# A hybrid token-mixer block on one core: recurrence products issued by shape and by alternating halves, and the first norm's sums of squares from a token-row copy of the input

## The chip, the cores and the metric

The kernel runs on one NeuronCore of one Trainium2 chip. The metric is device time in microseconds (us), lower is better. Engines are named as the profile names them: PE (TensorE matmul), PEld (its weight loads), DVE (VectorE), ACT (ScalarE), POOL (GpSimd), SP (SyncE, which issues nearly all DMAs).

## What is computed

One layer on x of 256 tokens by 2048 features, all in float32:

```python
h = rms_norm(x, attn_norm)                  # x * rsqrt(mean(x*x)) * g, per token
proj = h @ w_in                             # split into the inputs of four mixers and 4 gates
y_a = gla_mixer(...)                        # chunked gated linear attention
y_b = rglru_mixer(...)                      # conv + gated linear recurrence
y_c = nsa_mixer(...)                        # compressed / selected / window attention
y_d = rwkv7_mixer(...)                      # delta-rule recurrence, 8 heads of 64
merged = sum(sigmoid(gate_n) * (y_n @ w_branch[n]))
x = x + merged @ w_out
x = x + conv_ffn(rms_norm(x, ffn_norm))     # up 2 x 5632, causal conv of 3, silu gate, down
```

The recurrence that the change touches is rwkv7's, which the reference writes token by token and the kernel in four chunks of 64 tokens:

```python
sa = einsum('bhij,bhj->bhi', state, -kk_t)
state = state * w_t + sa[..., None] * (kk_t * a_t) + v_t[..., None] * k_t
y_t = einsum('bhij,bhj->bhi', state, r_t)
```

## The kernel before

Activations lie transposed, features on the 128 partitions and the 256 tokens along the free axis. Weights are streamed once from HBM by SP in pieces `raw` of 128x1024 (512 KB, five buffers). ACT casts each half to a rounded `wh`, DVE forms the rest `wl = raw - wh` (line 328; six buffers each), and `group_A` lets PE multiply both into a PSUM tile `acc`: for each 128-column block one product with 512 moving columns (`acc<-h,wh`) and one with 256 (`acc<-h,wl`). These two are the bulk of the program. The moving side `h` is the input times the norm's gain, split in the same way; the factor 1/rms of each token (`rs`) is multiplied in later, when an accumulator is read out (`scaled`).

The first weight group `r` goes into four PSUM tiles `r` that are read without that factor (`fold`), so `rs` is first needed some products later. `norm_sum` makes it from the pieces `xin` of the transposed input: ACT squares four pieces in place, POOL adds their quarters (lines 423 to 427, `TENSOR_TENSOR` on POOL, recorded under the helper's line 289), and `norm_fin` sums over partitions by a product with ones, takes root and reciprocal, and finally reduces `rs` back to one number per token row (`rstok`).

While the gate and branch products run, the chunks of the recurrence are woven between them. For each chunk `rwkv_pre` makes products `M` (keys against queries, masked into `mt`), and transposes `TK`; `rwkv_chain` makes `G` (from `mt` and `uv`, plus, after the first chunk, from the running state `st`), `U` (the triangular solve `Z` times `G`), `S` (the state update) and `Yo` (the output, again a part from `mt` and a part from `st`). Heads are paired on the partitions: `H` is the two halves 0..63 and 64..127, `j` counts four pairs. The part from `mt` is a product of 128 rows by 64 columns of the array, the part from `st` one of 64 by 64, and `M` one of 64 by 128. GLA has a like product `gy`. The accumulating pair of `G` is written as

```python
for j in range(4):
    for par in range(2):
        self.mm(ps[h, j, :], mt[:, par, j, 0:64], uv[:, j, par, :], start=True, stop=(st is None))
        if st is not None:
            self.mm(ps[h, j, :], ar[h, j, 0, :], st[h, j, :], start=False, stop=True)
```

The order on each engine is set by the framework's scheduler, which simulates a time line from the order of the code and from the bands of `at(...)` ("load" first, then "split", "evac", "mix", "big"). Engines run their queues strictly in that order. In the profile a float32 product of this kind is two matmul records.

Of the kernel before, what the change touches and what calls it, by code (L numbers as in the profile page):

```python
# [11 lines left out]
F32 = mybir.dt.float32  # L12
# [136 lines left out]
def _layout(i):  # L149
    a = {}  # L150
    a["xT"] = np.ascontiguousarray(i["x"][0].T.reshape(16, P, S).transpose(1, 0, 2))
# [74 lines left out]
class Kern:  # L226
# [190 lines left out]
    def norm_sum(self, src, acc=None, sq=None):  # L417

        nc = self.nc
        sq = self.sb("th", [P, 4, 256], F32, "sq") if sq is None else sq  # L420
# [9 lines left out]
    def norm_fin(self, red, tok):  # L430
# [10 lines left out]
        if tok:  # L441
            with self.at("mix"):
                d = self.m1("rsd", 2)
                self.tt(d, rs.rearrange("p (a t) -> p a t", a=2), self.cst("ident").unsqueeze(1).broadcast_to([P, 2, P]), MULT)
                self.rtok = self.sm([P, 2], "rstok")
                nc.vector.tensor_reduce(self.rtok, d, axis=mybir.AxisListType.X, op=ADD)
# [39 lines left out]
    def setup(self):  # L486
# [43 lines left out]
        self.consts = consts  # L530
        return xg
# [242 lines left out]
    def rwkv_pre(self, c, T):  # L774
# [5 lines left out]
        mask = self.cst("mM").unsqueeze(1).broadcast_to([P, 4, 128])  # L780
        for par in range(2):
            h = H[par]
            ps = self.ps("M")
            for j in range(4):
                self.mm(ps[:, j * 128:(j + 1) * 128], bk[h, j, par:par + 2, :].rearrange("p a b -> p (a b)"),
                        ar[h, j, :, :].rearrange("p a b -> p (a b)"))
            self.tt(mt[:, par], ps.rearrange("p (j t) -> p j t", j=4), mask, MULT)
# [14 lines left out]
        if c < 3:  # L802
# [5 lines left out]
            tk = self.sb("m2", [P, 2, 4, 64], F32, "tk")  # L808
            for par in range(2):
                h = H[par]  # L810
                ps = self.ps("TK")[:, 0:256].rearrange("p (j d) -> p j d", j=4)
                for j in range(4):
                    nc.tensor.transpose(ps[:, j, :], ht[h, j, par:par + 2, :].rearrange("p a b -> p (a b)"), idn[h, h])
                nc.scalar.copy(tk[:, par], ps)
# [3 lines left out]
    def rwkv_chain(self, c, T, st):  # L818
# [3 lines left out]
        g4 = lambda n: self.ps(n)[:, 0:256].rearrange("p (j s) -> p j s", j=4)  # L822
        ps = g4("G")
        for j in range(4):
            for par in range(2):
                h = H[par]
                self.mm(ps[h, j, :], mt[:, par, j, 0:64], uv[:, j, par, :], start=True, stop=(st is None))
                if st is not None:
                    self.mm(ps[h, j, :], ar[h, j, 0, :], st[h, j, :], start=False, stop=True)
# [24 lines left out]
        for j in range(4):  # L854
            for par in range(2):
                h = H[par]
                self.mm(ps[h, j, :], uv[:, j, par, :], mt[:, par, j, 64:128], start=True, stop=(st is None))
                if st is not None:
                    self.mm(ps[h, j, :], st[h, j, :], ar[h, j, 1, :], start=False, stop=True)
# [177 lines left out]
    def gla(self):  # L1037
# [28 lines left out]
        for lv in range(8):  # L1066
# [10 lines left out]
            if lv == 6:  # L1077
                for par in range(2):
                    h = H[par]
                    ps = self.ps("gy")[0:64, 0:256].rearrange("p (a t) -> p a t", a=4)  # L1080
                    for j in range(2):
                        for tl in range(2):
                            s0 = tl * 128
                            self.mm(ps[:, 2 * j + tl, :], qe[h, 2 + j, s0:s0 + 64], qe[h, j, s0 + 64:s0 + 128])
                    nc.vector.tensor_copy(st[par][0:64, :, 64:128], ps)
# [289 lines left out]
    def full(self, out):  # L1375
        nc = self.nc
        xg = self.setup()
# [99 lines left out]
        with self.at("evac"):  # L1477
            self.norm_fin(red, False)
# [75 lines left out]
```

## Time and profile before

| | |
|---|---|
| median of 3 runs | 1581.78 us (1580.47 to 1582.03) |
| profiled execution, its own time | 1582.63 us |
| its span on the core | 1580.8 us |
| PE, PEld, DVE, ACT, POOL busy | 99%, 89%, 78%, 61%, 2% of the span |
| TensorE clock granted, mean | 0.991 of full |
| moved by DMA | 305.79 MB, mean 193 GB/s |

The span is what the profiler sees of the core; the execution's own time is 1.83 us longer. Busy shares are means over stages with different limits. A busy PE can be running at half its clock, or be waiting inside itself between products, so its 99% doesn't say that the products take as long as they must.

### The profile page before, as it was taken

The numbers are of one execution on the slowest core, as the hardware profiler recorded it, in microseconds if no ns is written. First come the engines' busy times: TensorE is split into PE (matmuls) and PEld (weight loads), VectorE is DVE, ScalarE is ACT, GpSimd is POOL, SyncE is SP. The second block draws the span as 40 slices with busy tenths as digits, with TensorE's granted clock in tenths as the row PEclk, the third lists the DMA queues.
The fourth block names the chain that finished last, engine by engine and source line by source line (L and its number), as shares of the span: only waits on it lengthen the run. The fifth ranks groups of instructions, "written<-read, shape, count | busy, mean of one in ns | idle before, by whom it ended". The sixth has DMA issues, their size and how long they took to land.

```text
span 1580.8 us, 27481 instructions
## 1 busy us (share of the span) xinstructions
PE 1562.0 (99%) x10062; PEld 1413.0 (89%) x10062; DVE 1238.8 (78%) x2132; ACT 962.7 (61%) x1705; POOL 38.7 (2%) x60
## 2 busy tenths in 40 slices
PE   8999999999899999999999999999999999999998
PEld 7999888888799899899999999999999999999998
DVE  8799986476977677777787888886688886788875
ACT  6787654256665476656665666664466664566653
POOL 3000000000000000000001100000000000000000
PEclk9999999999999999999999999999999999999999
DMA  7756663245456755466676666666666666666664
GB/s 265 242 171 199 203 193 114 75 157 176 154 171 201 275 186 180 148 201 200 201 248 202 204 202 198 208 199 201 200 201 201 201 201 201 202 201 202 200 224 129
DMA packets 95800, 305.79 MB, mean 193 GB/s; under 512 B 20021, under 2 KB 20789, under 8 KB 95664
## 3 DMA queue, kind: packets, MB, share of 16 engines
q1 hardware_dynamic: 94448, 299.60, 59.9%
q0 software_dynamic: 1216, 4.43, 0.8%
q8 instruction: 79, 1.29, 0.3%
q14 instruction: 57, 0.47, 0.1%
HBM read 300.32 MB, written 3.67 MB: 192 GB/s over the span
## 4 chain that ended last, share of the span: by engine, by line
PE 95%; DVE 2%; ACT 1%; issue 1%; DMA 1%; SPq 0%; DVEq 0%; ACTq 0%
PE acc L297 89%; PE G L297 1%; PE Yo L297 1%; DVE wl L328 1%; DVE qe L289 0%; PE M L297 0%; PE no L297 0%; DMA raw<-in_wf_r 0%; PE r L297 0%; PE c L297 0%; ACT wh L327 0%; DVE th L289 0%; PE sc L297 0%; ACT ge L283 0%; PE ptp L1332 0%
## 5 line engine op out<-in xcount | busy, mean ns | idle before, releaser
L297 PE MATMUL acc<-h,wh 128*128 128x512 f32 x3008 | 1001.9, 385 | 3.0 <-DVE th L289 3.0
L327 ACT CAST wh<-raw 128x512 fp32r<-128x512 f32 x1096 | 673.6, 620 | 516.1 <-PE acc L297 490.8
L328 DVE TENSOR_TENSOR wl<-raw,wh 128x512 fp32r<-128x512 f32 x1096 | 757.7, 698 | 278.7 <-ACT wh L327 272.1
L297 PE MATMUL acc<-h,wl 128*128 128x256 f32 x3008 | 826.7, 275 | 0.0
L297 PEld LDWEIGHTS acc<-h,wh 128*128 128x128 f32 x3008 | 571.7, 190 | 85.3 <-DVE th L289 3.5
L297 PEld LDWEIGHTS acc<-h,wl 128*128 128x128 f32 x3008 | 580.5, 193 | 3.8 <-issue 1.6
L297 PE MATMUL acc<-f,wh 128*128 128x512 f32 x704 | 230.7, 382 | 0.0
L297 PE MATMUL acc<-f,wl 128*128 128x256 f32 x704 | 191.9, 273 | 0.0
L297 PEld LDWEIGHTS acc<-f,wh 128*128 128x128 f32 x704 | 133.1, 189 | 18.5
L297 PEld LDWEIGHTS acc<-f,wl 128*128 128x128 f32 x704 | 135.2, 192 | 0.0
L297 PE MATMUL acc<-mg,wh 128*128 128x512 f32 x256 | 83.9, 382 | 0.0
L286 DVE SCALAR_TENSOR_TENSOR u<-u,prm,u 128x254 f32<-128x254 f32 (+1 forms) x176 | 80.8, 480 | 0.5
L297 PE MATMUL acc<-mg,wl 128*128 128x256 f32 x256 | 69.5, 273 | 0.0
L297 PEld LDWEIGHTS acc<-mg,wh 128*128 128x128 f32 x256 | 48.2, 189 | 6.7
L289 DVE TENSOR_TENSOR xres<-xres,acc 128x512 f32<-128x512 f32 (+1 forms) x66 | 44.0, 668 | 10.0 <-PE acc L297 7.9
L283 ACT ACTIVATE u<-u,prm 128x256 f32<-128x256 f32 x88 | 48.1, 594 | 2.7 <-DVE u L289 0.8
L297 PEld LDWEIGHTS acc<-mg,wl 128*128 128x128 f32 x256 | 49.1, 192 | 0.1
L297 PE MATMUL acc<-wh,h 128*128 128x512 f32 (+1 forms) x128 | 32.2, 340 | 0.0
L289 DVE TENSOR_TENSOR u<-u,rs 128x512 f32<-128x512 f32 x44 | 30.1, 684 | 0.0
L289 DVE TENSOR_TENSOR u<-u,acc 128x512 f32<-128x512 f32 x44 | 29.9, 680 | 0.0
L380 ACT COPY u<-acc 128x512 f32<-128x512 f32 x44 | 25.5, 579 | 0.0
L297 PEld LDWEIGHTS acc<-wh,h 128*128 128x128 f32 x128 | 23.2, 202 | 2.1 <-issue 0.4
(399 smaller groups left out, 1240.9 us busy)
## 6 DMA issues: line engine op xcount, KB each, us to landing
raw<-in_w_up SPq DMA_DIRECT2D x176, 512.0 KB, 4.2
raw<-in_w_gate SPq DMA_DIRECT2D x128, 512.0 KB, 4.0
raw<-in_w_down SPq DMA_DIRECT2D x88, 512.0 KB, 4.3
raw<-in_w_branch SPq DMA_DIRECT2D x32, 512.0 KB, 3.8
raw<-in_w_out SPq DMA_DIRECT2D x32, 512.0 KB, 4.4
raw<-in_wf_k SPq DMA_DIRECT2D x8, 512.0 KB, 4.6
raw<-in_wf_misc SPq DMA_DIRECT2D x8, 512.0 KB, 4.0
raw<-in_wf_lx SPq DMA_DIRECT2D x8, 512.0 KB, 4.2
```

What stands on the lines that cost most here:

```text
L283: return self.nc.scalar.activation(out, in_, func, bias=bias, scale=scale, **kw)
L286: return self.nc.vector.scalar_tensor_tensor(out, in0, scalar, in1, op0=op0, op1=op1)
L289: return (eng or self.nc.vector).tensor_tensor(out, a, b, op=op)
L297: return self.nc.tensor.matmul(out, lhsT, rhs, start=start, stop=stop, **kw)
L327: nc.scalar.copy(wh, rb)
L328: nc.vector.tensor_tensor(wl, rb, wh.bitcast(F32), op=SUB)
L380: self.nc.scalar.copy(dst, ps[0:rows, :, 0])
```

## The change

It has two parts, delivered together.

**Order of products.** In `G` and `Yo` all products from `mt` are issued first and all products from `st` after them, instead of in pairs; in `M`, `TK` and `gy` the two halves of the partitions alternate, instead of one half's four products before the other's, so both PSUM tiles of the pair are open at once. The products are the same.

**First norm.** Instead of squaring the transposed pieces on ACT and adding them on POOL, four pieces `xtok` of the input with tokens on the partitions (128x1024 each, 2 MB more from HBM) are loaded, and ACT squares them with a running sum along the row. The root and reciprocal are taken on two numbers per partition; a diagonal matrix of them times ones spreads them to `rs`. The eleven POOL additions of this norm are gone, as are a root and a reciprocal of 128x256.

```diff
+    a["x"] = np.ascontiguousarray(i["x"][0].reshape(2, P, 2, 1024).transpose(0, 2, 1, 3)).reshape(4, P, 1024)
...
+    def norm_tok(self):
+        nc = self.nc
+        ss = self.sm([P, 2, 2], "sstok")
+        for n, t in enumerate(self.xtok):
+            self.act(t, t, AF.Square, accum_out=ss[:, n // 2, n % 2:n % 2 + 1])
+        self.rtok = self.sm([P, 2], "rstok")
+        nc.vector.tensor_reduce(self.rtok, ss, axis=mybir.AxisListType.X, op=ADD)
+        self.act(self.rtok, self.rtok, AF.Sqrt, scale=1.0 / D, bias=self.cst("eps6"))
+        nc.vector.reciprocal(self.rtok, self.rtok)
+        d = self.m1("rsd", 2)
+        for tt in range(2):
+            self.ts(d[:, tt, :], self.cst("ident"), self.rtok[:, tt:tt + 1], None, MULT)
+        ps = self.ps("ss")
+        with self.at("big"):
+            self.mm(ps[:, 0:256], self.cst("ones"), d.rearrange("p a t -> p (a t)"))
+        rs = self.pools["c"].tile([P, 256], F32, tag="rs", bufs=1, name=f"rs_{self.nt}")
+        nc.scalar.copy(rs, ps[:, 0:256])
...
+        def tokens():
+            self.xtok = []
+            for n in range(4):
+                t = self.sb("m4", [P, 1024], F32, "xtok")
+                with self.at("load"):
+                    nc.sync.dma_start(t, A["x"][n])
+                self.xtok.append(t)
...
-                            red = None
-                            for g in range(4):
-                                red = self.norm_sum(xg[g], red, xg[g])
-                            self.norm_fin(red, True)
+                            self.norm_tok()
...
-                    self.extras = [self.consts, lambda: None, norm]
+                    self.extras = [self.consts, self.tokens, norm]
...
+        pm = [self.ps("M") for _ in range(2)]
+        for j in range(4):
+            for par in range(2):
+                h = H[par]
+                self.mm(pm[par][:, j * 128:(j + 1) * 128], bk[h, j, par:par + 2, :].rearrange("p a b -> p (a b)"),
+                        ar[h, j, :, :].rearrange("p a b -> p (a b)"))
         for par in range(2):
-            h = H[par]
-            ps = self.ps("M")
-            for j in range(4):
-                self.mm(ps[:, j * 128:(j + 1) * 128], bk[h, j, par:par + 2, :].rearrange("p a b -> p (a b)"),
-                        ar[h, j, :, :].rearrange("p a b -> p (a b)"))
...
+        heads = [(j, par, H[par]) for j in range(4) for par in range(2)]
         ps = g4("G")
...
+        for j, par, h in heads:
+            self.mm(ps[h, j, :], mt[:, par, j, 0:64], uv[:, j, par, :], start=(j == 0), stop=(st is None), skip_group_check=True)
+        if st is not None:
+            for j, par, h in heads:
+                self.mm(ps[h, j, :], ar[h, j, 0, :], st[h, j, :], start=False, stop=True, skip_group_check=True)
...
+        for j, par, h in heads:
+            self.mm(ps[h, j, :], uv[:, j, par, :], mt[:, par, j, 64:128], start=(j == 0), stop=(st is None), skip_group_check=True)
+        if st is not None:
+            for j, par, h in heads:
+                self.mm(ps[h, j, :], st[h, j, :], ar[h, j, 1, :], start=False, stop=True, skip_group_check=True)
```

What the scheduler makes of it shows at three places. The first is PE's queue at the `G` of the second chunk; `G` from `uv` and `mt` is the part from the mask, `G` from `st` and `ops` the part from the state. Before:

```order
L813 MATMUL TK_3250<-cstt,ht_3240 128x64 x4
L297 MATMUL G_3256<-uv_3146,mt_3133 64x64
L297 MATMUL G_3256<-st_3204,ops_1045 64x64
L297 MATMUL G_3256<-uv_3146,mt_3133 64x64
L297 MATMUL G_3256<-st_3204,ops_1045 64x64
L297 MATMUL G_3256<-uv_3146,mt_3133 64x64
L297 MATMUL G_3256<-st_3204,ops_1045 64x64
```

Now, at the same place:

```order
L837 MATMUL TK_3239<-cstt,ht_3235 128x64 x2
L837 MATMUL TK_3240<-cstt,ht_3235 128x64 x2
L837 MATMUL TK_3239<-cstt,ht_3235 128x64
L837 MATMUL TK_3240<-cstt,ht_3235 128x64
L837 MATMUL TK_3239<-cstt,ht_3235 128x64
L837 MATMUL TK_3240<-cstt,ht_3235 128x64
L298 MATMUL G_3251<-uv_3141,mt_3128 64x64 x8
L298 MATMUL G_3251<-st_3199,ops_1040 64x64 x8
```

The sixteen products that went in eight pairs now go in two runs of eight; the transposes `TK` ahead of them alternate only in part.

The second place is PE's queue where the second chunk's state and output (`S`, `Yo`), the fourth chunk's `M` and the third chunk's `G` meet. Before:

```order
L297 MATMUL S_3286<-uv_3146,tk_3160 64x64
L297 MATMUL Yo_3299<-mt_3133,uv_3146 64x64
L297 MATMUL Yo_3299<-ops_1045,st_3204 64x64
L297 MATMUL M_3318<-ops_1059 128x128 x2
L297 MATMUL S_3286<-uv_3146,tk_3160 64x64 x7
L297 MATMUL Yo_3299<-mt_3133,uv_3146 64x64
L297 MATMUL Yo_3299<-ops_1045,st_3204 64x64
L297 MATMUL Yo_3299<-mt_3133,uv_3146 64x64
```

Now:

```order
L298 MATMUL S_3281<-uv_3141,tk_3155 64x64
L298 MATMUL Yo_3294<-mt_3128,uv_3141 64x64
L298 MATMUL M_3313<-ops_1054 128x128 x3
L298 MATMUL S_3281<-uv_3141,tk_3155 64x64 x7
L298 MATMUL Yo_3294<-mt_3128,uv_3141 64x64 x7
L298 MATMUL Yo_3294<-ops_1040,st_3199 64x64 x8
L298 MATMUL M_3314<-ops_1054 128x128 x3
L298 MATMUL M_3313<-ops_1054 128x128
L298 MATMUL M_3314<-ops_1054 128x128
L298 MATMUL G_3336<-uv_3224,mt_3211 64x64 x8
L298 MATMUL G_3336<-st_3290,ops_1047 64x64 x8
```

The sixteen rows of `Yo`, which alternated, now stand in runs of one shape, as does `G`. Before, the rest of `M` and six rows of `acc` stood between this `Yo` and the third chunk's `G`; now only `M` does, and its halves alternate only in the last three rows. The first chunk's `M` alternates throughout, the second's after two runs of two, the third's like the fourth's.

The third place is ACT's queue at the end of the weight group `r`, with the last piece of its weights, `raw_330`, and before it the four squares. Before:

```order
L283 ACTIVATE xin_226<-xin_226 128x1024
L327 CAST wh_300<-raw_298 128x512
L327 CAST wh_312<-raw_298 128x512
L283 ACTIVATE xin_291<-xin_291 128x1024
L327 CAST wh_332<-raw_330 128x512
```

Now:

```order
L328 CAST wh_300<-raw_298 128x512
L328 CAST wh_312<-raw_298 128x512
L284 ACTIVATE xtok_395,sstok_429<-xtok_395 128x1024
L284 ACTIVATE xtok_397,sstok_429<-xtok_397 128x1024
L284 ACTIVATE xtok_399,sstok_429<-xtok_399 128x1024
L284 ACTIVATE xtok_401,sstok_429<-xtok_401 128x1024
L284 ACT_TABLE_LOAD
L284 ACTIVATE rstok_434<-rstok_434,eps 128x2
L328 CAST wh_332<-raw_330 128x512
```

The squares, spread over the group before, now stand together ahead of the casts of its last piece, with a table load and the root. On SP's queue the four loads of `xtok` stand between `raw_298` and `raw_330`.

## Rows read from the trace of the kernel before

**Rows 1.** The page: PE's busy time; the chain that ended last.

```profile
PE 1562.0 (99%) x10062; PEld 1413.0 (89%) x10062; DVE 1238.8 (78%) x2132; ACT 962.7 (61%) x1705; POOL 38.7 (2%) x60
...
PE 95%; DVE 2%; ACT 1%; issue 1%; DMA 1%; SPq 0%; DVEq 0%; ACTq 0%
```

**Rows 2.** Busy time by stretch (columns in the first line): recurrence, and the stretch before it.

```profile
core 0: us, PE busy (x) PEld busy (x) DVE busy (x) ACT busy (x) POOL busy (x), PEclk, DMA share, GB/s
160.00:200.00 40.00, 38.42 (x235) 35.11 (x234) 39.83 (x79) 26.21 (x44) 0.00 (x0) 1.00 0.66 206
240.00:280.00 40.00, 40.00 (x314) 34.20 (x313) 25.83 (x51) 17.30 (x35) 0.61 (x2) 0.92 0.35 109
280.00:320.00 40.00, 40.00 (x301) 32.48 (x301) 17.38 (x35) 11.11 (x23) 1.17 (x3) 0.91 0.27 84
```

**Rows 3.** PE's time line, paired products: start, us, operation, array rows*columns, count.

```profile
266.02 0.33 PE L297 MATMUL G<-uv,mt 128*64 128x64 f32 x2
266.28 0.33 PE L297 MATMUL G<-st,ops 64*64 64x64 f32 x2
...
270.13 0.79 PE L297 MATMUL acc<-h,wh 128*128 128x512 f32 x1
...
270.93 0.63 PE L297 MATMUL acc<-h,wh 128*128 128x512 f32 x1
...
281.33 0.33 PE L297 MATMUL Yo<-ops,st 64*64 64x64 f32 x2
```

**Rows 4.** PE's time line, runs of one shape, and two rows of the bulk.

```profile
243.30 1.71 PE L297 MATMUL M<-ops 64*128 64x128 f32 x16
...
249.25 0.69 PE L297 MATMUL G<-uv,mt 128*64 128x64 f32 x16
...
250.18 0.27 PE L297 MATMUL acc<-h,wl 128*128 128x256 f32 x1
250.29 0.38 PE L297 MATMUL acc<-h,wh 128*128 128x512 f32 x1
250.51 0.27 PE L297 MATMUL acc<-h,wl 128*128 128x256 f32 x1
...
253.55 0.68 PE L297 MATMUL U<-G,Z 64*64 64x64 f32 x16
```

**Rows 5.** Stretches after the paired G, first and last of three (columns as in Rows 2).

```profile
269.60:274.00 4.40, 4.40 (x19) 3.76 (x18) 0.42 (x1) 0.99 (x2) 0.00 (x0) 0.61 0.08 34
...
310.50:314.90 4.40, 4.40 (x19) 3.75 (x19) 1.20 (x2) 1.48 (x3) 0.00 (x0) 0.61 0.00 0
```

**Rows 6.** PE's time line at two ends of the group r.

```profile
10.17 1.13 PE L297 MATMUL r<-h,wh 128*128 128x512 f32 x4 [0.83 <-ACT wh L327]
...
35.62 0.61 PE L297 MATMUL r<-h,wl 128*128 128x256 f32 x4
```

**Rows 7.** The start: PE's waits to 60 us, and wl in it (min/median/max ns).

```profile
PE r L297 <- DVE wl L328: 3.8, 4, 2.3
...
L328 DVE TENSOR_TENSOR wl<-raw,wh x9: 676/678/3947, 26.4 to 35.0; 128x512 fp32r<-128x512 f32 x9
```

**Rows 8.** Stretches of the start (columns as in Rows 2).

```profile
0.00:20.00 20.00, 17.02 (x76) 14.03 (x77) 14.71 (x45) 14.59 (x29) 4.96 (x11) 1.00 0.86 318
10.00:20.00 10.00, 8.88 (x50) 7.70 (x51) 9.78 (x21) 9.45 (x20) 4.37 (x4) 1.00 1.03 412
25.00:30.00 5.00, 2.89 (x17) 1.98 (x15) 5.00 (x5) 3.47 (x6) 3.86 (x6) 1.00 0.61 192
```

**Rows 9.** ACT's groups: count, busy us, mean ns, idle before.

```profile
L327 ACT CAST wh<-raw 128x512 fp32r<-128x512 f32 x1096 | 673.6, 620 | 516.1 <-PE acc L297 490.8
...
L283 ACT ACT_TABLE_LOAD x18 | 23.1, 1283 | 0.6 <-issue 0.3
...
L283 ACT ACTIVATE xin<-xin 128x1024 f32<-128x1024 f32 x4 | 4.2, 1058 | 2.8 <-DVE h L286 2.8
...
L283 ACT ACTIVATION_READ_ACCUMULATOR pt<-pt,nm 128x1 f32 x16 | 3.0, 187 | 0.0
```

More of the change, by code (lines that the diff above doesn't have):

```diff
@@ L415, in norm_split, with norm_sum @@
             self.stt(dst[:, a, 1, :], src[:, a, :], gn, dst[:, a, 0, :].bitcast(F32), MULT, SUB)
-    def norm_sum(self, src, acc=None, sq=None):
+    def norm_sum(self, src, acc=None):
         nc = self.nc
-        sq = self.sb("th", [P, 4, 256], F32, "sq") if sq is None else sq
+        sq = self.sb("th", [P, 4, 256], F32, "sq")
         self.act(sq, src, AF.Square)
@@ L428, in norm_sum, with norm_fin @@
         return red
-    def norm_fin(self, red, tok):
+    def norm_tok(self):
[15 more added lines that the diff above has]
+        nc.scalar.copy(rs, ps[:, 0:256])
+        self.rs = rs
+        self.rs4 = rs.unsqueeze(1).broadcast_to([P, 4, 256])
+    def norm_fin(self, red):
         nc = self.nc
@@ L440, in norm_fin @@
         self.rs4 = rs.unsqueeze(1).broadcast_to([P, 4, 256])
[L441 to L446, printed above, removed]
     def scaled(self, t, ps, rows=P):
@@ L528, in consts @@
             self.load_after(self.hl[7][0:1, 1, 1, 0:1], self.cstt, A["cst"])
-        self.consts = consts
-        return xg
+        def tokens():
[5 more added lines that the diff above has]
+                self.xtok.append(t)
+        self.consts, self.tokens = consts, tokens
     def shift_evac(self, dst, ps, mu0, n, rows=P):
@@ L780, in rwkv_pre @@
         mask = self.cst("mM").unsqueeze(1).broadcast_to([P, 4, 128])
-        for par in range(2):
-            h = H[par]
-            ps = self.ps("M")
-            for j in range(4):
-                self.mm(ps[:, j * 128:(j + 1) * 128], bk[h, j, par:par + 2, :].rearrange("p a b -> p (a b)"),
-                        ar[h, j, :, :].rearrange("p a b -> p (a b)"))
-            self.tt(mt[:, par], ps.rearrange("p (j t) -> p j t", j=4), mask, MULT)
+        pm = [self.ps("M") for _ in range(2)]
[4 more added lines that the diff above has]
+                        ar[h, j, :, :].rearrange("p a b -> p (a b)"))
+        for par in range(2):
+            self.tt(mt[:, par], pm[par].rearrange("p (j t) -> p j t", j=4), mask, MULT)
         T["mt"] = mt
@@ L808, in rwkv_pre @@
             tk = self.sb("m2", [P, 2, 4, 64], F32, "tk")
-            for par in range(2):
[L810 to L814, printed above, removed]
+            pt = [self.ps("TK")[:, 0:256].rearrange("p (j d) -> p j d", j=4) for _ in range(2)]
+            for j in range(4):
+                for par in range(2):
+                    h = H[par]
+                    nc.tensor.transpose(pt[par][:, j, :], ht[h, j, par:par + 2, :].rearrange("p a b -> p (a b)"), idn[h, h])
+            for par in range(2):
+                nc.scalar.copy(tk[:, par], pt[par])
             T["tk"] = tk
@@ L822, in rwkv_chain @@
         g4 = lambda n: self.ps(n)[:, 0:256].rearrange("p (j s) -> p j s", j=4)
+        heads = [(j, par, H[par]) for j in range(4) for par in range(2)]
         ps = g4("G")
[L824 to L829, printed above, removed]
+        for j, par, h in heads:
[3 more added lines that the diff above has]
+                self.mm(ps[h, j, :], ar[h, j, 0, :], st[h, j, :], start=False, stop=True, skip_group_check=True)
         g = self.m1("G")
@@ L853, in rwkv_chain @@
         ps = g4("Yo")
[L854 to L859, printed above, removed]
+        for j, par, h in heads:
[3 more added lines that the diff above has]
+                self.mm(ps[h, j, :], st[h, j, :], ar[h, j, 1, :], start=False, stop=True, skip_group_check=True)
         nc.scalar.copy(self.rw_y[:, :, c * 64:c * 64 + 64], ps)
@@ L1077, in gla @@
             if lv == 6:
-                for par in range(2):
[L1079 to L1085, printed above, removed]
+                py = [self.ps("gy")[0:64, 0:256].rearrange("p (a t) -> p a t", a=4) for _ in range(2)]
+                for j in range(2):
+                    for tl in range(2):
+                        s0 = tl * 128
+                        for par in range(2):
+                            h = H[par]
+                            self.mm(py[par][:, 2 * j + tl, :], qe[h, 2 + j, s0:s0 + 64], qe[h, j, s0 + 64:s0 + 128])
+                for par in range(2):
+                    nc.vector.tensor_copy(st[par][0:64, :, 64:128], py[par])
             elif lv < 6:
@@ L1376, in full @@
         nc = self.nc
-        xg = self.setup()
+        self.setup()
         hk = self.pairs(self.hl)
@@ L1477, in full @@
         with self.at("evac"):
-            self.norm_fin(red, False)
+            self.norm_fin(red)
         h2 = self.pairs(h2)
```

## The prediction

> **What bounds the kernel now.** I read the page first: PE is busy 99% of the span and makes up 95% of the chain that ended last [rows 1]. So time is won only where PE's products take longer than they must, or where PE stands still. The table of stretches says where the first holds. From 240 to 320 us PE is busy all 80 us, yet DVE is busy for only 26 and 17 of 40, the loads run at about half of what they reach elsewhere, and the granted clock is 0.92 and 0.91 [rows 2]: nothing feeds PE late there, PE itself is slow. These are the chunks of the recurrence.
>
> PE's time line shows why. The paired products of G change shape at each step (128 by 64, then 64 by 64), and the second row starts 0.26 us after the first; the sixteen rows run from 266.02 to 270.13, 4.11 us [rows 3]. In runs of one shape sixteen records of the same products take 0.69 us (first chunk's G, 128 by 64) and 0.68 us (U, 64 by 64, halves alternating) [rows 4]. Yo's pairs have the same 0.33 us per row as G's [rows 3]. Behind the paired G the bulk product takes 0.63 us [rows 3] instead of 0.38 [rows 4]: PE is at 1.2 GHz instead of 2.4. That happens three times, each a stretch of 4.40 us with a mean clock of 0.61 [rows 5].
>
> The start is the second place. Group r has sixteen steps, each of four pairs; a pair of bulk products takes 0.33 us (250.18 to 250.51) [rows 4], a step 1.32. The third step starts at 10.17, and the last one's last four products start at 35.62 [rows 6] and take four times 0.11 us [rows 4]; less one 0.22 us product of the next group that stands between, that is an end at 35.84. Fourteen steps took 25.7 us instead of 18.5; 7.2 us are lost. PE waited 3.8 us there for DVE's wl, and of nine wl with a median of 678 ns one took 3947 [rows 7], in a stretch in which POOL was busy for 3.86 of 5 us and DVE for all 5 [rows 8]. POOL's additions for the norm hold DVE up; the rest of the 7.2 us is the restarts, a lower clock behind the longest wait, and ACT.
>
> **The change, part by part.**
>
> *G and Yo by shape.* Six blocks are paired before (chunks two to four, G and Yo; the first has no part from the state). Each goes from 4.11 us to 0.69 + 0.68 = 1.37 [rows 3, 4], with one change of shape left inside. 6 x 2.74 = **16.4 us**. The difference over 30 changes of shape is 0.09 us a change, which I use below.
>
> A rule of the Trainium skill speaks against this term. The row first: U writes both halves of the partitions into one PSUM tile, and its sixteen records take 0.68 us [rows 4], no slower than G's 0.69 with all 128 rows. The page "TensorEngine Tiling (Array Packing)", section "Gotcha 1: PSUM Pressure", says that different row tiles cannot access the same PSUM bank at the same time. By it the run from the state would go half by half, at the 1.71 us that M's sixteen need, and the sum would be 6 x 1.03 = 6.2 us smaller; the trace does not agree, so I go by the row and keep the rule as a rival.
>
> *The clock.* Three falls follow the three paired G blocks. A stretch of 4.40 us at 0.61 loses 0.39 x 4.40 = 1.72 us [rows 5]; three are **5.1 us**. No run of one shape is followed by one in these rows (the acc product after the first chunk's G takes 0.38 at 250.29 [rows 4]), so I take all three as gone. Bounds: 0, if the closer-packed clusters (S, Yo, M, G in one piece, some 4 us by the prices above) do the same; 6.8, if a fourth fall elsewhere goes too.
>
> *M by halves.* No row has 64 by 128 products with alternating halves. Bounds for one record: 0.107 as now (1.71 / 16) and 0.043 as in U [rows 4]. I take 0.055, which is what 128 moving columns cost in the bulk (256 take 0.11 [rows 4]), since U streams only half as many: 16 x 0.05 = 0.8 us for a block that alternates at all seven places. The scheduler keeps 7, 5, 3 and 3 of the 28, so 18 / 7 x 0.8 = 2.0, less two new changes of shape where M's first run enters between two S: **1.8 us** (0 to 2.5). TK alternates in part and gy has eight products; both are counted as nothing, 0.3 either way.
>
> *The first norm.* ACT's four squares of 1.06 us and POOL's additions leave the group. DVE's wl then takes 0.68 us and, with two of them and two shorter splits per piece, less than PE's 2.64 us a piece; PE would go at its own pace and end r at 10.17 + 18.5 = 28.7. What is late next is the last piece. By 20.0 us the loads moved 318 GB/s x 20 us = 6.4 MB [rows 8], which is all of r's weights (4.2), the transposed input (2.1) and the parameters. The four new loads of 2.1 MB now stand ahead of the last piece, and at 412 GB/s [rows 8] push it by 5.1 us: the last xtok lands at 20.0 - 1.3 + 5.1 = 23.8 (the 1.3 is the last piece itself), the piece at 25.1. Behind that xtok ACT has a square (1.06), a wait for DVE's sum of four numbers (0.3, an estimate), a table load (1.28) and the root (0.2, an estimate), and only then the cast that PE waits for (0.62) [rows 9]: 27.3. PE wants it twelve steps after 10.17, at 26.0. So the squares hold the casts for 1.3 us, r ends at 30.0, and the gain is **5.8 us**. Bounds: 7.2 if the loads come early enough, 0 if the piece comes 5.8 us later than this. The diagonal product costs what the old one did; the old reciprocal of 128x256 leaves DVE.
>
> *Whether it stays won.* From 160 to 200 us DVE is busy 39.83 of 40 [rows 2]; if only PE came earlier, the gain at the start would be waited away there. DVE comes earlier too, since it was the one that POOL held. In the recurrence DVE is idle for 37 of 80 us, and U stands 22 rows of acc, 3.6 us, behind its G, which covers ACT's copy. I take nothing off, and up to 2 us for the range.
>
> Sum: 16.4 + 5.1 + 1.8 + 5.8 = 29.1 us off the profiled execution's own 1582.63, so 1553.5. The median is 0.85 us lower than that execution, so **1553 us**.
>
> **Rivals.**
>
> *The clock still falls.* The clusters hold few dense products; for it: the falls came after four microseconds of such work. Against: the runs keep the array about three times as busy as the pairs. All three back: 1553 + 5 = 1558.
>
> *The loads eat the start.* For it: in the first 20 us the DMA engines are fully taken, share 1.03 from 10 to 20 us [rows 8], and what is put ahead delays the rest. If the last piece lands at about 31 (2.1 MB at some 190 GB/s), the start gains nothing: 1559.
>
> *Banks.* The rule above: 1559. Against it stands U.
>
> *The change doesn't do what it says.* If products of 64 columns cost 0.26 us by themselves and not by the change of shape, only the start is won: 1553 + 16.4 + 5.1 + 1.8 = 1576. Rows 4 speak against it for both shapes.
>
> *Slower: the hand-offs.* A chunk goes from PE to ACT or DVE and back at G to U, U to S, and S to the next G, eleven times in all. In the new order the third and fourth chunks' G follow their S with no acc between. Each hand-off is covered by 1.5 to 3.9 us of other products. PE would stand still for what exceeds it; to pass 29 us the mean excess must be over 2.6 us, that is hand-offs of some 6 us. Against: PE is busy for all of 240 to 320 us now [rows 2], with DVE idle for 37 of the 80 us and ACT for 52. Just past that point it is 1586.
>
> **How the numbers follow.** Chances: forecast 0.66, clock 0.14, loads 0.12, banks 0.04, no effect of order 0.02, hand-offs 0.02. A difference under 0.2% (3.2 us) is about what a measurement of this kernel cannot tell from none. All cases but the last are faster by more than that; I leave 0.01 for cases that meet in the middle. The low end takes the upper bounds: M 0.7 more, the start 1.4, a fourth fall 1.7, which gives 1549, and 1 us for TK and gy and the spread of runs: 1548. The high end takes in the clock and the loads, and part of both: 1561. That leaves out under 2 in 10.
>
> **What would show it.** In the profile after: the second chunk's G as two rows of sixteen records, 0.7 us each; granted clock 1.00 instead of 0.92 and 0.91 over the recurrence; M's first block near 0.9 us, its third near 1.4; no wl near 4 us at the start; r's last product near 30 us, after a wait of some 1.3 us for ACT's cast behind the squares. I am wrong if G's or Yo's runs stay above 1 us each, if PE begins to wait between 230 and 330 us, if the last piece of r lands past 28 us, or if the start's gain is there at 40 us and gone at 220.

## The result, and the profile after

| | before | after |
|---|---|---|
| median | 1581.12 us (1577.91 to 1582.03) | 1553.64 us (1551.99 to 1554.62) |
| ratio | | 0.9822, 95% interval 0.98 to 0.9844 |
| profiled execution, its own time | 1582.63 us | 1551.99 us |
| span | 1580.8 us | 1550.2 us |
| granted clock, mean | 0.991 | 0.999 |

One execution of the changed kernel and one of an experiment (M kept in order), of 4.5 ms each, lie outside all others; medians, ranges and ratios here leave them out (with it, the changed kernel's median is 1554.13 us). The forecast was 1553, in a range of 1548 to 1561. The total fits, but not term by term.

The page of the changed kernel answers to [rows 1]: PE is still the whole of it, busy for 30.2 us less.

```profile
PE 1531.8 (99%) x10062; PEld 1391.6 (90%) x10062; DVE 1229.0 (79%) x2133; ACT 963.7 (62%) x1710; POOL 27.0 (2%) x49
...
PE 95%; DVE 2%; DMA 1%; issue 1%; ACT 0%; SPq 0%; DVEq 0%; ACTq 0%
```

The table of stretches after: first the recurrence, to be held against [rows 2], then the start, against [rows 8], and last the stretch around GLA's `gy`, which lies 27 us earlier than before (at 398.4 instead of 425.5).

```profile
core 0: us, PE busy (x) PEld busy (x) DVE busy (x) ACT busy (x) POOL busy (x), PEclk, DMA share, GB/s
240.00:280.00 40.00, 40.00 (x403) 35.23 (x402) 31.71 (x65) 19.57 (x39) 1.22 (x4) 1.00 0.43 144
280.00:320.00 40.00, 40.00 (x340) 34.79 (x339) 27.90 (x46) 23.11 (x42) 0.86 (x2) 1.00 0.49 149
25.00:30.00 5.00, 1.21 (x8) 0.94 (x8) 0.92 (x3) 4.58 (x9) 0.00 (x0) 1.00 1.03 414
30.00:35.00 5.00, 5.00 (x22) 4.43 (x21) 4.53 (x11) 3.80 (x10) 0.00 (x0) 0.66 0.76 264
396.00:408.00 12.00, 8.90 (x67) 7.69 (x66) 11.35 (x21) 9.41 (x19) 0.54 (x1) 1.00 0.41 142
```

The clock in the recurrence is 1.00 where it was 0.92 and 0.91, and DVE and the loads do more in the same 40 us. At the start, PE works for 1.21 of 5 us and then runs at a clock of 0.66.

Two more stretches of the kernel before, which its rows above don't hold, lost clock as well:

```profile
236.00:244.00 8.00, 7.71 (x66) 6.29 (x66) 7.71 (x17) 2.96 (x7) 0.00 (x0) 0.79 0.27 89
424.00:436.00 12.00, 9.15 (x48) 7.99 (x48) 10.45 (x20) 7.60 (x15) 0.54 (x1) 0.72 0.46 143
```

The second one holds `gy`, with a wait of 1.4 us before it and one behind it. The changed kernel waits there as well (1.4 and 1.7 us), and its clock is 1.00. That is not the work of the new orders: the kernel with the orders alone, in its second run below, has the same queue and the same waits there and loses as much as the kernel before.

```profile
396.00:408.00 12.00, 8.91 (x49) 7.73 (x48) 10.49 (x20) 7.58 (x15) 0.54 (x1) 0.72 0.46 147
```

The first one comes and goes too: the norm alone, with the old orders, has a clock of 1.00 from 232 to 244 us, and `G` paired, with the new order of `M`, has 0.79 from 228 to 236 us, ahead of any paired block.

PE's time line after, at the start, at the first `M` and at the second chunk's `G`, which answers to [rows 3, 4, 6]:

```profile
29.43 1.13 PE L298 MATMUL r<-h,wh 128*128 128x512 f32 x4 [3.79 <-ACT wh L328]
30.39 0.82 PE L298 MATMUL r<-h,wl 128*128 128x256 f32 x4
...
32.72 1.06 PE L298 MATMUL r<-h,wl 128*128 128x256 f32 x4
...
230.67 1.16 PE L298 MATMUL M<-ops 64*128 64x128 f32 x16
...
262.58 0.69 PE L298 MATMUL G<-uv,mt 128*64 128x64 f32 x16
263.20 0.68 PE L298 MATMUL G<-st,ops 64*64 64x64 f32 x16
263.81 0.38 PE L298 MATMUL acc<-h,wl 128*128 128x256 f32 x1
264.02 0.38 PE L298 MATMUL acc<-h,wh 128*128 128x512 f32 x1
```

`G` starts at 262.58 and the bulk goes on at 263.81: 1.23 us instead of 4.11. The second `acc` product behind it, with 512 columns, takes 0.38 us, so PE is at 2.4 GHz there. `r` ends at 32.72 + 4 x 0.21 = 33.6, not at 30.0, behind a wait of 3.79 us instead of 1.3.

ACT's time line shows that wait from the other side. The four squares stand in front of the casts of `r`'s last piece:

```profile
22.39 1.06 ACT L284 ACTIVATE xtok<-xtok 128x1024 f32<-128x1024 f32 x1 [0.42 <-DMA xtok<-in_x]
23.36 0.19 ACT L284 ACTIVATION_READ_ACCUMULATOR xtok<-xtok 128x1 f32 x1
24.57 1.06 ACT L284 ACTIVATE xtok<-xtok 128x1024 f32<-128x1024 f32 x1 [1.03 <-DMA xtok<-in_x]
...
25.86 1.06 ACT L284 ACTIVATE xtok<-xtok 128x1024 f32<-128x1024 f32 x1
...
27.28 1.28 ACT L284 ACT_TABLE_LOAD   x1 [0.27 <-DVE rstok L438]
28.57 0.29 ACT L284 ACTIVATE rstok<-rstok,eps 128x2 f32<-128x2 f32 x1
28.77 3.21 ACT L328 CAST wh<-raw 128x512 fp32r<-128x512 f32 x6
```

The list of loads issued from 12.5 to 17.5 us (count, KB each, median us from issue to landing) and SP's queue tell when the data were there:

```profile
xtok<-in_x SPq DMA_DIRECT2D x4, 512.0 KB, 9.2
raw<-in_wf_r SPq DMA_DIRECT2D x1, 512.0 KB, 10.2
...
16.94 0.33 SPq L321 DMA_DIRECT2D raw<-in_wf_r  x1
```

The last piece of `r` landed at 16.94 + 10.2 = 27.1 and not at 25.1. What held `r` before is gone: the longest `wl` to 40 us takes 693 ns, where it was 3947 [rows 7].

```profile
L329 DVE TENSOR_TENSOR wl<-raw,wh x26: 681/685/693, 4.3 to 39.8; 128x512 fp32r<-128x512 f32 x26
```

### The profile page after: what moved, and what is told of

The parts are those of the page before. It is cut to its first block, busy times and chain, and to the rows that moved or that the text cites. A ratio compares the mean times of both kernels' runs of the same rounds, so it can differ in the third digit from the quotient of the medians.

```text
span 1550.2 us, 27484 instructions
## 1 busy us (share of the span) xinstructions
PE 1531.8 (99%) x10062; PEld 1391.6 (90%) x10062; DVE 1229.0 (79%) x2133; ACT 963.7 (62%) x1710; POOL 27.0 (2%) x49
## 4 chain that ended last, share of the span: by engine, by line
PE 95%; DVE 2%; DMA 1%; issue 1%; ACT 0%; SPq 0%; DVEq 0%; ACTq 0%
PE acc L298 90%; DMA raw<-in_wf_k 1%; DVE wl L329 1%; DVE qe L290 0%; DMA raw<-in_cmp 0%; PE no L298 0%; PE M L298 0%; PE c L298 0%; PE Yo L298 0%; DVE th L290 0%; DMA raw<-in_wf_r 0%; PE r L298 0%; PE sc L298 0%; PE G L298 0%; ACT ge L284 0%
## 5 line engine op out<-in xcount | busy, mean ns | idle before, releaser
L298 PE MATMUL acc<-wh,h 128*128 128x512 f32 (+1 forms) x128 | 30.6, 328 | 0.0
L284 ACT ACTIVATE th<-th 128x512 f32<-128x512 f32 (+1 forms) x33 | 21.2, 644 | 4.9 <-DVE th L290 4.9
```

The source lines that it names most:

```text
L284: return self.nc.scalar.activation(out, in_, func, bias=bias, scale=scale, **kw)
L298: return self.nc.tensor.matmul(out, lhsT, rhs, start=start, stop=stop, **kw)
```

## The experiments

All were timed beside the kernel before on the same chip, in three groups of four. Orders alone (first time), norm alone, `G` paired and the late loads stood on one chip, where the kernel before has a median of 1579.97 us; the other two groups stood on a second chip, where it has 1583.34 us (the changed kernel again, the old order of `M`, the state part by halves, late and spread) and 1581.21 us (the other four).

| kernel | median us (range) | ratio to before (95%) |
|---|---|---|
| orders alone, first time | 1553.15 (1552.38 to 1553.45) | 0.9821 (0.9799 to 0.9844) |
| orders alone, again | 1553.53 (1551.77 to 1554.66) | 0.982 (0.9796 to 0.9844) |
| the changed kernel again | 1553.72 (1552.04 to 1556.53) | 0.982 (0.9801 to 0.984) |
| norm alone | 1584.68 (1580.33 to 1588.84) | 1.0022 (1.0007 to 1.0038) |
| G paired again | 1568.66 (1560.46 to 1574.25) | 0.9911 (0.9884 to 0.9938) |
| Yo paired again | 1565.87 (1561.6 to 1570.04) | 0.9899 (0.9874 to 0.9924) |
| M, TK, gy in the old order | 1557.73 (1553.83 to 1560.25) | 0.9841 (0.9818 to 0.9865) |
| state part half by half | 1559.09 (1558.19 to 1559.34) | 0.985 (0.9831 to 0.987) |
| token loads late | 1550.03 (1548.85 to 1553.11) | 0.9806 (0.9781 to 0.983) |
| token loads late and spread | 1548.56 (1546.23 to 1551.67) | 0.9787 (0.9766 to 0.9808) |
| the same, M kept in order | 1549.92 (1546.09 to 1552.04) | 0.9802 (0.9778 to 0.9826) |
| orders alone, POOL's sums left out | 1546.75 (1546.31 to 1547.55) | 0.9779 (0.9756 to 0.9802) |

**The two parts apart.** The first kernel has the new orders and the old norm:

```diff
-        self.norm_tok()
+        red = None
+        for g in range(4):
+            red = self.norm_sum(xg[g], red, xg[g])
+        self.norm_fin(red, True)
```

> Only the product orders are changed; the first norm is that of the kernel before. By the trace of the changed kernel (theory A: the start won only about 2 us, the orders the rest, with more clock back than forecast): about 26 us less than before, 1555 to 1556, group r ending near 35.8 us as before and no half-clock stretch from 215 to 325 us nor at 425 to 434. By the terms as forecast (theory B: 16.4 + 5.1 + 1.8 = 23.3 for the orders, 5.8 for the norm): 1558. If the two parts depend on each other (theory C: the earlier start is what keeps the waits out of the recurrence), waits of PE appear between 160 and 330 us and the time is over 1560.

The second has the new norm and the old `rwkv_pre`, `rwkv_chain` and `gy`.

> Only the first norm is changed; G, Yo, M, TK and gy go in the order of the kernel before. Theory A: 1579, about 2 us less than before, with the same wait of some 3.8 us for the cast behind the squares and the half clock behind it, and the three half-clock stretches after the paired G still there. Theory B (as forecast): 1575. Theory C (the start's gain is waited away later when DVE is the limit from 160 to 200 us): 1581, no change, with more PE idle time from 160 to 240 us.

The orders alone take 1553.15 us, 2 to 3 less than theory A and 5 less than the forecast's terms. With the norm added it is 1553.64 to 1553.72: the norm was worth nothing. Norm alone is not 2 us faster but slightly slower than the kernel before, which none of the three theories expected. Its start is the one of the changed kernel (a wait of 3.4 us, `r` ending at 33.2), and its waits from 160 to 240 us are longer by only 0.3 us in all, so theory C falls too. What is longer is the half clock in the recurrence; its table of stretches:

```profile
264.00:272.00 8.00, 8.00 (x50) 6.48 (x51) 1.12 (x2) 1.61 (x3) 0.00 (x0) 0.79 0.27 83
284.00:296.00 12.00, 12.00 (x73) 9.79 (x72) 2.45 (x4) 2.74 (x6) 0.00 (x0) 0.72 0.16 44
300.00:316.00 16.00, 16.00 (x93) 12.44 (x93) 2.82 (x6) 3.23 (x7) 0.00 (x0) 0.79 0.17 45
```

The second and third fall cost 3.4 us each (0.28 x 12, 0.21 x 16), twice what they cost before [rows 5]. Over all its executions the mean clock is 0.987 to 0.991, against 0.988 to 0.995 for the kernel before. Why an earlier start goes with longer falls is not settled.

The orders alone were timed once more, in the last group.

> The orders alone once more, beside the version of this call. 1553 again, r's last product at 34 to 36 us (35.8 with a half-clock stretch behind DVE's late wl, 34 without). If the first measurement was low by chance: 1555 to 1556.

It is 1553.53 us, with the last four products of `r` at 33.68, as in the first run, so they end at 34.1. Neither run has a half clock there; the profiled execution of the kernel before has one, and ended at 35.84.

The changed kernel was run again in the second group.

> The changed kernel once more, beside the three others of this call, since the kernel with the orders alone came out at 1553.15 us on another chip. If the new norm is worth nothing (theory H: its gain on POOL and DVE is paid back by the wait behind the squares): 1553 to 1555 again, no less than the orders alone, with a wait of 3.5 to 5 us for the cast near 25.5 us and half clock behind it. If the first measurement was high by chance: 1551, as the start 2 us earlier than in the kernel before would give.

Theory H holds: 1553.72 us, a wait of 3.55 us behind the squares and half clock behind it.

**The late token loads.** The four loads wait for the last piece of the input's split, so that they stand behind `r` on SP's queue and the squares behind `r` on ACT's:

```diff
-                with self.at("load"):
-                    nc.sync.dma_start(t, A["x"][n])
+                self.load_after(self.hl[7][0:1, 1, 1, 0:1], t, A["x"][n])
```

> The changed kernel with the four token loads made to wait for the last piece of the split input, which puts them on the load queue behind the last piece of r and three pieces of k, and the squares on ACT behind r's casts. Theory A (the squares and the late last piece cost the start 3.8 us of wait and about 1.7 us of half clock): group r ends near 28.7 to 29.5 us and the time is 1549 to 1550, 4 to 5 us less than the changed kernel. Rival D (the loads only move the hole: the pieces of k come 5 us late and PE waits for them): r ends early, PE waits 3 to 5 us for k's casts between 30 and 45 us, and the time stays at 1554. Rival E (what is won at the start is waited away where DVE is the limit, from 160 to 200 us): 1553 to 1554 with PE idle there.

1550.03 us, 3.1 less than the orders alone beside it: theory A, with a piece of rival D, one wait of 1.45 us for `k`'s cast at 38.39 us. The next version takes that wait away by spreading the loads over the first pieces of `k`:

```diff
-        def tokens():
+        def tokens(dep, ns):
-            for n in range(4):
+            for n in ns:
...
+                self.load_after(dep, t, A["x"][n])
...
-                    self.extras = [self.consts, self.tokens, norm]
+                    self.extras = [first, lambda: self.tokens(self.wl[0:1, 0:1], (1,)), norm]
```

`first` loads the constants and `tokens(..., (0,))`, and `norm` begins with `tokens(self.wl[0:1, 0:1], (2, 3))`; `self.wl` is the latest split.

> The version with the token loads behind r, with the four loads spread between the pieces of k (each waits for a later split) instead of in one piece. The late version still waited 1.45 us near 38 us for k's cast, behind four squares, a table load and a root in one row on ACT. Theory: that wait goes too, group r ends near 29 us, PE has no wait from 11 to 150 us, and the time is 1548 to 1549. Rival (the scale of the tokens comes too late for the first read-out of k, so that the accumulators are held): PE waits for an accumulator near 50 us, and the time is 1550 or more.

1548.56 us, as expected, 5.2 less than the changed kernel beside it. The squares now lie between 29 and 41 us on ACT, and PE is busy without a gap from 26 to 40 us:

```profile
29.19 1.09 ACT L284 ACTIVATE xtok<-xtok 128x1024 f32<-128x1024 f32 x1
...
40.00 1.06 ACT L284 ACTIVATE xtok<-xtok 128x1024 f32<-128x1024 f32 x1
...
42.19 1.28 ACT L284 ACT_TABLE_LOAD   x1
```

```profile
26.00:40.00 14.00, 14.00 (x88) 12.90 (x87) 9.18 (x17) 10.74 (x22) 1.75 (x5) 1.00 1.02 412
```

**What held DVE at the start.** The orders alone, with POOL's additions left out (one squared piece stands for the sum):

```diff
         g = nc.gpsimd
+        if src is sq:
+            return sq[:, 0, :]
         self.tt(sq[:, 0:2, :], sq[:, 0:2, :], sq[:, 2:4, :], ADD, g)
```

> The orders alone with the norm of the kernel before, but POOL's eleven additions of the first norm are left out (the last piece's squares stand for their sum, so the norm's value is another); ACT's squares stay. Theory (POOL's additions hold DVE's wl, not ACT's squares): no wl over 0.7 us before 40 us, r's last product near 29 us instead of 34, and 1548 to 1549, 4 to 5 us less than the orders alone. Rival M (ACT's four squares and DVE's own load make the 7 us): r ends at 32 us or later and the time is 1552.

1546.75 us, 6.8 less than with them. The `wl` to 40 us, first with POOL's additions (orders alone, again), then without:

```profile
L328 DVE TENSOR_TENSOR wl<-raw,wh x25: 673/678/3970, 4.2 to 38.6; 128x512 fp32r<-128x512 f32 x25
```

```profile
L328 DVE TENSOR_TENSOR wl<-raw,wh x28: 628/683/693, 4.2 to 39.4; 128x512 fp32r<-128x512 f32 x28
```

PE's last four products of `r` start at 27.65 instead of 33.68. ACT's squares are in both, so rival M falls. The Trainium skill, page "SBUF — State Buffer", section "🔬 SBUF: two separate sides", says that a DVE operation with two SBUF inputs and a GpSimd operation that reads SBUF need one port pair under an exclusive lock, and that the one that comes later is fully blocked; the 3970 against 693 ns agree.

**The paired blocks.** `G` alone back in pairs:

```diff
-        for j, par, h in heads:
-            self.mm(ps[h, j, :], mt[:, par, j, 0:64], uv[:, j, par, :], start=(j == 0), stop=(st is None), skip_group_check=True)
-        if st is not None:
-            for j, par, h in heads:
-                self.mm(ps[h, j, :], ar[h, j, 0, :], st[h, j, :], start=False, stop=True, skip_group_check=True)
+        for j in range(4):
+            for par in range(2):
+                h = H[par]
+                self.mm(ps[h, j, :], mt[:, par, j, 0:64], uv[:, j, par, :], start=True, stop=(st is None))
+                if st is not None:
+                    self.mm(ps[h, j, :], ar[h, j, 0, :], st[h, j, :], start=False, stop=True)
```

> The changed kernel with G alone put back into pairs; Yo stays by shape. Theory A (changes of shape cost 0.09 us each, and the thin paired blocks are what the clock falls after): G's three blocks 4.11 us each again, 3 x 2.74 = 8.2 us, and three half-clock stretches of 1.7 us behind them, 5.1 us: 1567. Rival F (the clock falls came from the whole thin cluster around G, which is shorter now): 8.2 us alone and clock 1.00 over 240 to 320 us: 1562. Rival G (the falls followed M's or TK's same-half runs): also 1562, and no bulk product at 0.63 us behind a paired G.

`Yo` alone likewise.

> The changed kernel with Yo alone put back into pairs, G by shape. Cost by shape: 3 x 2.74 = 8.2 us as for G: 1562 with clock 1.00. Theory K (any paired block of four microseconds brings the half clock, since it starts within the block after some three microseconds in the kernel with paired G): half-clock records inside or right behind Yo's pairs in most blocks, 1567 to 1570, and scattered times, 10 us apart. Rival L (it is G's place, behind TK or M, that matters): 1562 with clock 0.998 and times within 4 us.

With `G` paired the six executions lie at 1560.46 to 1574.25 us, and the fastest is the one with a mean clock of 0.999. Executions of `G` by shape with that clock took 1552.04 us (the changed kernel again, on the other chip) and 1553.07 to 1553.45 us (orders alone, on the same chip): the block's price is 7.0 to 8.4 us (8.2 forecast), and the rest is clock. With `Yo` paired the fastest two, at a clock of 0.998, are 7.6 to 8.2 us over the changed kernel's executions with that clock (1553.43 and 1554.01). In the time line of paired `G` the fall can be seen inside the block:

```profile
270.69 0.33 PE L298 MATMUL G<-uv,mt 128*64 128x64 f32 x2
270.95 0.32 PE L298 MATMUL G<-st,ops 64*64 64x64 f32 x2
271.21 0.47 PE L298 MATMUL G<-uv,mt 128*64 128x64 f32 x2
271.61 0.47 PE L298 MATMUL G<-st,ops 64*64 64x64 f32 x2
...
273.19 0.63 PE L298 MATMUL acc<-h,wh 128*128 128x512 f32 x1
...
274.47 0.63 PE L298 MATMUL acc<-h,wh 128*128 128x512 f32 x1
```

The step from row to row goes from 0.26 to 0.40 us among products that have not changed, and the dense `acc` that follows is still at 0.63. So 1.2 GHz comes with the paired block itself, not only with the cluster around it (rivals F and G fall), though not in each execution: the fastest one has a mean clock of 0.999. For `Yo`, theory K holds in part: the profiled execution has such a stretch behind one of its three paired blocks, at 292 to 300 us.

One rival has no experiment of its own: in a pair, the second product adds to the place that the first has just written, so the price could be a wait for that write and not the change of shape. A place in the changed kernel's trace speaks against it. There one product of `Yo` stands alone between two `acc`, which write elsewhere, and it takes the same 0.26 us as a row of the pairs [rows 3]:

```profile
297.32 0.38 PE L298 MATMUL acc<-h,wh 128*128 128x512 f32 x1
297.63 0.33 PE L298 MATMUL Yo<-mt,uv 128*64 128x64 f32 x2
297.89 0.38 PE L298 MATMUL acc<-h,wl 128*128 128x256 f32 x1
```

**M by halves.** The old order of `M`, `TK` and `gy` within the changed kernel: `for par` outside `for j`, one PSUM tile after the other.

> The changed kernel with M, TK and gy in the old order, four products of one half and then four of the other; G and Yo stay by shape. By the trace of the changed kernel the alternation is worth 0.5 us per fully alternating block of M and about nothing in the two split ones: 1555. Theory I (the half-clock stretches at 236 to 244 and 424 to 436 us of the kernel before, which no paired G precedes, came from these same-half runs): these two come back, 1.7 and 3.1 us, and the time is near 1559. Rival J (they depend on the paired blocks or on chance): clock 1.00 in both stretches and 1555. By the terms as forecast: 1553 + 1.8 = 1555 as well, with the M blocks 1.71 us each.

1557.73 us, 4.0 over the changed kernel. The spans of the two profiled executions differ by 4.4 us. Two `M` blocks that take 1.64 us instead of 1.25 and 1.14, from their first record to the next product, are 0.89 of it. Most of the rest is clock, in its table of stretches:

```profile
26.00:40.00 14.00, 10.74 (x47) 9.55 (x48) 8.79 (x20) 9.63 (x19) 0.00 (x0) 0.76 0.80 295
404.00:408.00 4.00, 4.00 (x16) 3.48 (x15) 4.00 (x8) 2.90 (x6) 0.01 (x1) 0.57 0.49 186
```

The first costs (0.88 - 0.76) x 14 = 1.7 us more than in the changed kernel, whose clock is 0.88 there, with the same queues; the second, at `gy`, costs 1.7. That second one is also in the orders alone, with `gy` alternating (0.64 from 400 to 404 us in one execution, 0.50 in the other), so it doesn't follow from the order of halves; the other one, at 236 to 244 us, did not come back. So theory I falls, and these falls come in some executions and not in others.

Last, `M` kept in program order in the version with the spread loads, so that each block alternates and stands in one piece:

```diff
-                self.mm(pm[par][:, j * 128:(j + 1) * 128], bk[h, j, par:par + 2, :].rearrange("p a b -> p (a b)"),
+                m = self.mm(pm[par][:, j * 128:(j + 1) * 128], bk[h, j, par:par + 2, :].rearrange("p a b -> p (a b)"),
...
+                if c:
+                    self.tc.keep_in_program_order(m)
```

> The version with the token loads spread behind r, and M's products of the second to fourth chunk kept in program order, so that each block alternates halves throughout and stands in one piece behind Yo instead of split around S. Theory (an alternating block is 1.16 us; the split blocks cost about 2.1, the same-half runs and two changes of shape more): 0.9 us less in the third and fourth block each, 1.8 in all: 1546.8. Rival (the earlier first products of M were filler for a wait of PE before S or G): PE waits for ACT or DVE between 240 and 300 us, and the time is 1548.5 or more.

The blocks are 1.16 us in one piece, where the split ones take 0.93 and 1.16 with `S` and `Yo` between, but the median of five is 1549.92, and the spans of the profiled executions are 1544.3 and 1544.5. That is 0.2 us and not the 1.8 that I expected, and this run doesn't tell it from nothing.

**Halves within the state part.** The part from the state half by half:

```diff
-            for j, par, h in heads:
+            for par, j in [(p, j) for p in range(2) for j in range(4)]:
+                h = H[par]
                 self.mm(ps[h, j, :], ar[h, j, 0, :], st[h, j, :], start=False, stop=True, skip_group_check=True)
```

> The changed kernel with the part from the state of G and Yo issued half by half (four products of the lower half, then four of the upper), still behind the part from the mask. It prices the alternation of halves inside a run of 64 by 64 products. Theory: a record that follows one of the same half takes 0.107 us as in M's old order, against 0.043 when halves alternate: six runs of 0.68 become 1.7 us each, 6 us in all: 1560, with clock 1.00. Rival (64 moving columns make no difference between the halves): the runs stay at 0.7 us, 1554. Rival (the longer, thinner clusters bring the half clock back behind G): over 1562.

```profile
266.55 0.69 PE L298 MATMUL G<-uv,mt 128*64 128x64 f32 x16
267.17 0.96 PE L298 MATMUL G<-st,ops 64*64 64x64 f32 x16
```

The run takes 0.96 us instead of 0.68: 0.28 x 6 = 1.7 us, between theory and rival. The measured 5.4 us have more in them, and it doesn't come from these products: the profiled execution is 4.0 us late already at the first `M` (234.65 instead of 230.67), by half clock behind `r`'s wait and longer waits from 160 to 230 us, in queues that are the same. Why all four executions lie there stays open.

## Why the prediction was right, and where it was not

*G and Yo by shape* (16.4 us): right. A block went from 4.11 to 1.23 us, 17.3 for six by the rows, and undoing one of the two costs 7.0 to 8.4 us at equal clock, where 8.2 were forecast. The rival that the order does nothing falls. The price of one change was miscounted, though. Sixteen rows in pairs change shape fifteen times and not thirty, and fourteen changes are gone: 2.88 / 14 = 0.21 us each, not 0.09. Not all of that is the change, since in the pairs the two halves of the array don't overlap either: half by half, the run from the state takes 0.28 us more. If the run from the mask did the same (an estimate from that run), 0.56 of a block's 2.88 us would be the halves and 2.3 the changes, 0.17 each.

The rival of the banks falls too: the run from the state takes 0.68 us with both halves in one bank. The Trainium skill, page "TensorEngine Tiling (Array Packing)", section "Gotcha 1: PSUM Pressure", has it that different row tiles cannot access the same PSUM bank simultaneously. The trace doesn't agree where the halves write different partitions of it, as `U`, `G` and `Yo` do; halves that write the same partitions of one bank were not run. The 6.2 us that I had put on this rival were too high as well: half by half the run takes 0.96 us, not 1.71.

*The clock* (5.1 us): the mechanism is right, and for the three stretches behind `G` the size too: 3 x 1.7 = 5.1 us, gone in the profile after. The two profiled executions differ by 10.1 us of clock, but the other 5.0 (0.21 x 8 at 236 to 244 us, 0.28 x 12 at `gy`) fell at places where a fall comes and goes with the execution, as shown above; between these two executions they are luck. What I had not seen is that every fall is a matter of the execution: on one chip the kernel before took 1576.93 us at a mean clock of 0.995 and 1586.49 at 0.988. A straight line through its executions puts it at about 1570 us with the clock at 1.00 (seventeen on the first chip, ten on the second) or 1567.5 (seven on the second), and the changed kernel's four at 1550.7. These are estimates from result times and a clock known to a thousandth. By them 17 to 19 of the 27.5 us between the medians are products and start, and 8 to 11 are clock.

*M by halves* (1.8 us): too high. In the middle of an alternating block two records, one of each half, start every 0.112 us, so a record takes 0.056, as I had it (by the starts of the single records in the trace). But the old order was not 0.107 throughout: there three records of the second half start beside records of the first, where the halves meet, and the first and the last step of a block don't get shorter. From the first record to the next product a block went from 1.64 to 1.25 and 1.14 us: 0.9 us for the first two. In the third and fourth the split around `S` and `Yo` used it up.

*The first norm* (5.8 us): wrong. The step that failed is "the last xtok lands at 23.8 ... the piece at 25.1". The piece landed at 27.1, since loads issued into full queues took 9 to 10 us, where the last loads of `r` took 6.7 in the kernel before; the last square started at 25.86 instead of 23.8. At the 414 GB/s of that stretch the 2 us are 0.8 MB that came ahead of the piece. Three pieces of `k` were issued right behind it, from 17.62 us; that they took this share is likely, but no run shows it. The chain behind the last square was sized well: 3.5 us from its start to the end of the cast, as forecast, so that the cast that PE waited for was done at 29.4 instead of 27.3. PE stood still from 25.6, and "the squares hold the casts for 1.3 us" became 3.79. The 1.7 us of half clock behind the wait (0.12 x 14, 26 to 40 us) were not in the sum. `r` ended at 33.6. Against the orders alone, 34.1, that is half a microsecond, and in the times nothing. The cause that I gave for the loss was right: POOL's additions cost 6.8 us. They were taken away, and a wait behind the squares and loads took their place. The rival "the loads eat the start" is what happened, by squares and loads together, without the piece landing past 28 us as I had put it.

*Whether it stays won:* it does. The version with late, spread loads starts `r`'s last `wl` product at 28.07, so it ends `r` some 5 us before the changed kernel does, and its total is 5.2 us less.

Of the profiled execution's 30.6 us, 17.3 are G and Yo, 10.1 clock, 0.9 M and 2.2 the start: 30.5. The forecast's 29.1 were right in sum by luck: the start was too high by 3.6 and M by 0.9, and 5.0 us of clock came from falls that the one execution happened to have and the other not. Of the measured median's gain the norm has nothing.

## What to carry to other kernels

Products that change their shape at each step cost the change (about 0.2 us each here, with the overlap of the halves that goes with it) and can take the clock with them: put equal shapes together, and judge by several executions, since the clock falls in some and not in others. The fall at `gy` would have passed for a gain of the change if the same queue had not shown it in another kernel. Work that is moved off a busy engine is won only if its new place is not in front of something awaited: ask where its loads stand in the load queue and where its instructions stand in the new engine's queue. Here the same norm was worth nothing ahead of the last piece of `r` and 5.2 us behind it.

## What the hardware showed that I had not expected

The clock fell in the middle of a block of sixteen rows, and stayed at 0.63 us per dense product for several more. In kernels with paired blocks the executions of one kernel scatter by 4 to 14 us on a chip, and the slower ones mostly have the lower mean clock; without paired blocks they scatter by 1.1 to 6.4 us.

Alternating the halves halves the time of a record, but not that of a block. 64 by 128 products start every 0.112 us on one half and two at a time in the same 0.112 us when the halves alternate; 64 by 64 ones every 0.058 us on one half and two at a time in 0.058. A block of sixteen gains less, 1.64 to 1.25 or 1.14 us and 0.89 to 0.61, because its first and last steps stay and the old order overlaps where the halves meet.
